# Where weights stand in TensorE: a high product of 512 columns as two of 256 in one half bank

## The chip, the cores and the metric

The kernel runs on one core of one Trainium2 chip. The metric is the device time of one execution in microseconds, given as the median of several runs; lower is better. One execution was also recorded by the profiler, and everything said about engines comes from that one.

## The reference

One decoder layer on 256 tokens of width 2048, in float32. Cut to what matters:

```python
h = rms_norm(x, g_mix)
z = h @ w_in                      # 2048 -> pool 512 | q-latent 512 | kv-latent 256 | rope key 64 | memory query 512
y = concat(pool_mixer(z_pool), mla(z_q, z_kv, z_kr), mem_attention(z_mq, mem)) @ w_o
x = x + y
h = rms_norm(x, g_ffn)
g, u = h @ w_gate, h @ w_up       # 2048 -> 5632 each
gc = conv_b + sum_j conv_w[j] * shift(g, j)        # causal, width 3
x = x + (silu(gc) * u) @ w_down   # 5632 -> 2048
```

## The kernel before

Every operand of a large product is split into two float32r parts, high and low, where low is the rest that high leaves. A product a x b is computed as high x high + high x low + low x high; the fourth term is left out. Weights arrive by DMA in blocks of 1 MB (load_w, tile wr) and are split by split_w: ACT casts to wh (L98), DVE subtracts to wl (L99), in pieces of 128 x 1024. Activations are split in the same way by split_act, and their high and low parts stand beside each other: xg[:, k, 0:256] and [256:512] in the input stage, h2[:, 0, k] and h2[:, 1, k] in the feed-forward stage.

There are two manners of product. In gemm_n (the memory keys and values, the query and rope key, the up-projections, the output projection) and in prod (the down-projection) the activations stand in TensorE as the stationary operand and weights stream past, mostly 512 columns. In gemm_t, gemm_z and gemm_pair the weights stand and the activations stream past: these three are where the change is. Their output is 128 features by 256 tokens, and a bank of PSUM has room for 512 columns. For each of the 16 blocks k of the inner dimension,

- a *high* product streams both parts of the activations, 512 columns, past the high weights: the product with high activations goes into the first half of the bank, that with low activations into the second half;
- a *low* product streams the high part of the activations, 256 columns, past the low weights into the second half.

The helper sides picks output and moving operand for both. Afterwards the two halves are added: ACT copies the first half to SBUF and DVE adds the second, in half_add (L509, L510, tile hadd) in the input stage and in halves (L809, L810, tiles g and u) in the feed-forward stage.

The stages in order of time, by the profile: the memory product, where memory keys and values are made (to about 50 us); the query and rope key (50 to 77 us); six latent blocks with gemm_z (L140), between whose high and low runs the steps of the memory attention are put (77 to 126 us); four pool blocks, the first with gemm_z and three with gemm_t (L124), among the up-projections (126 to 182 us); attention heads beside the output projection (to 288 us); the feed-forward stage; the down-projection (771 to 996 us).

The feed-forward stage loops over f, 44 blocks of 128 features. Each f takes two banks, for gate and up. The first f is done in two halves by gemm_t, with other work between. The other 43 use gemm_pair (L156): the gate's 16 high products, its 16 low ones, then the up's 16 low ones and its 16 high ones, so that runs of one kind meet, also across two f: TensorE sees 32 low, 32 high, 32 low, and so on. Then glu makes the result on ACT and DVE: add the halves of the gate, multiply by the row scale r1 (L815), convolve (L817, L819), silu (L820), add the halves of the up part, multiply (L826 or L834), split.

A scheduler places the instructions on each engine by dependency and priority; where keep() is called, they stay in the order of the program. Matmuls and splits of gemm_pair are not kept. Banks come from a pool of four (ps_main), the parts of weights from pools of four buffers each. The tile of the low weights has 64 spare columns, and its start is shifted by 48 columns for the first half of a block of weights and by 16 for the second.

Of the kernel before, what the change touches and what calls it, by code (L numbers as in the profile page):

```python
# [60 lines left out]
def layer(ctx, tc, xT_d, xn_d, memT_d, vec_d, tab_d, w_z_d, w_mqkr_d, w_q_d, w_kv_d, w_mem_d, w_pool_d, w_o_d,  # L61
          w_g_d, w_u_d, w_dn_d, out_d):
    nc = tc.nc
# [24 lines left out]
    def keep(ins, on=True):  # L88

        return tc.keep_in_program_order(ins) if on else ins  # L90
# [18 lines left out]
    def gemm_t(ps, raw, o, act, ks, first=True, last=True, kept=False, between=None):  # L109


        ks = list(ks)
        nk = HS // P
        cs = range(0, len(ks), nk)
        for c in cs:
            kc = ks[c:c + nk]

            hi, lo = split_w(raw, o + c * P, len(kc) * P, shift=16 if c // nk % 2 else 48)

            for low in ((False, True) if c // nk % 2 == 0 else (True, False)):  # L120
                for i, k in enumerate(kc):
                    w = (lo if low else hi)[:, i * P:(i + 1) * P]
                    out, m = sides(ps, act(k), low)
                    keep(nc.tensor.matmul(out, w, m,  # L124
                                          start=first and c + i == 0 and not low,
                                          stop=last and c == cs[-1] and i == len(kc) - 1 and low == (c // nk % 2 == 0),
                                          skip_group_check=True), kept)
            if between is not None and c == 0:
                between()

    def gemm_z(ps, raw, act, between, low_first):


        nk = HS // P
        parts = [split_w(raw, c * HS, HS, shift=16 if c else 48) for c in range(KD // nk)]
        for low in ((True, False) if low_first else (False, True)):
            for k in range(KD):
                i = k % nk
                o, m = sides(ps, act(k), low)
                keep(nc.tensor.matmul(o, parts[k // nk][low][:, i * P:(i + 1) * P], m, start=k == 0 and low == low_first,  # L140
                                      stop=k == KD - 1 and low != low_first, skip_group_check=True))
            if low == low_first:
                between()

    def gemm_pair(pss, raws, act):

        nk = HS // P
        for s, (ps, raw) in enumerate(zip(pss, raws)):


            parts = [split_w(raw, c * HS, HS, shift=16 if c else 48) for c in range(KD // nk)]
            for low in ((False, True) if s == 0 else (True, False)):
                for k in range(KD):
                    i = k % nk
                    o, m = sides(ps, act(k), low)
                    nc.tensor.matmul(o, parts[k // nk][low][:, i * P:(i + 1) * P], m,  # L156
                                     start=k == 0 and low == (s == 1), stop=k == KD - 1 and low == (s == 0),
                                     skip_group_check=True)

    def gemm_n(pss, hi, lo, act, k0, first, last, kept=False, by_span=False):  # L160

# [29 lines left out]
    def v(name, i=0):  # L191
        o = VOFF[name] + i
        return vec[:, o:o + 1]
# [309 lines left out]
        if m == 6:  # L503
            latent_scales()

    def half_add(dst, ps):

        t = mp.tile([P, T], F32, tag="hadd", name=nm("hadd"), bufs=3)
        nc.scalar.copy(t[:], ps[:, 0:T])  # L509
        nc.vector.tensor_tensor(dst, t[:], ps[:, T:2 * T], op=ALU.add)  # L510


    zl = mp.tile([P, 6, 2 * T], F32R, name="zl")
    zs = mp.tile([P, 2, T], F32, name="zs")

# [2 lines left out]
    for m in range(6):  # L518
        raw = load_w(w_z_d[m], STG)
        if m in (1, 3):  # L520
            keep(nc.sync.dma_start(x1n[:, m // 2, :], xn_d[m // 2]))
        ps = ps_main()
        gemm_z(ps, raw, lambda k: xg[:, k, :], lambda: mem_steps(m), m % 2 == 1)
        z = mp.tile([P, T], F32, tag="hadd", name=nm("z"), bufs=3)
        half_add(z[:], ps)
        a = zs[:, m // 4, :]
        if m % 4 == 0:
            nc.scalar.activation(a, z[:], AF.Square)
        else:
# [3 lines left out]
        split_act(zl[:, m, :], z[:], v("g_q_lat", m) if m < 4 else v("g_kv_lat", m - 4))  # L533


    sl, sl2 = sm(4), sm(4)
# [15 lines left out]
    zp = mp.tile([P, 4, T], F32, name="zp")  # L552
    def pool_in(g):
        raw = load_w(w_z_d[6 + g], STG)
        ps = ps_main()
# [247 lines left out]
    aT = {}  # L803
    hold = {}

    def halves(ps, tag):

        t = fp.tile([P, T], F32, tag=tag, name=nm(tag), bufs=1)
        nc.scalar.copy(t[:], ps[:, 0:T])  # L809
        nc.vector.tensor_tensor(t[:], t[:], ps[:, T:2 * T], op=ALU.add)  # L810
        return t

    def glu(f, psg, psu):
        g = halves(psg, "g")
        nc.vector.tensor_tensor(g[:], g[:], r1[:], op=ALU.mult)  # L815
        gc = fp.tile([P, T], F32, tag="gc", name=nm("gc"), bufs=1)
        nc.scalar.activation(gc[:], g[:], AF.Identity, bias=v("conv_b", f), scale=v("cw2", f))  # L817
        for d, w in ((1, "cw1"), (2, "cw0")):
            nc.vector.scalar_tensor_tensor(gc[:, d:T], g[:, 0:T - d], v(w, f), gc[:, d:T], op0=ALU.mult, op1=ALU.add)  # L819
        nc.scalar.activation(gc[:], gc[:], AF.Silu)  # L820
        u = halves(psu, "u")
        j, e = f // 2, f % 2
        if j not in SEVEN:
            if e == 0:
                aT[j] = fp.tile([P, 2, 2 * T], F32R, name=nm("aT"))
            nc.vector.tensor_tensor(u[:], u[:], gc[:], op=ALU.mult)  # L826
            split_act(aT[j][:, e, :], u[:])
            return
        if e == 0:
# [4 lines left out]
        nc.vector.tensor_tensor(s[:, o:o + 2, :].rearrange("p a t -> p (a t)"), u[:], gc[:], op=ALU.mult)  # L834
# [8 lines left out]


    raws = [load_w(w[0], STG) for w in (w_g_d, w_u_d)]
    pss = [ps_main() for _ in range(2)]
    for ps, raw in zip(pss, raws):
        gemm_t(ps, raw, 0, lambda k: h2[:, :, k, :], range(8), last=False)
    turn(3)
# [4 lines left out]
        gemm_t(ps, raw, HS, lambda k: h2[:, :, k, :], range(8, KD), first=False)  # L854
    glu(0, *pss)
    for f in range(1, KF):
        pss = [ps_main() for _ in range(2)]
        gemm_pair(pss, [load_w(w[f], STG) for w in (w_g_d, w_u_d)], lambda k: h2[:, :, k, :])
        glu(f, *pss)

# [191 lines left out]
```

## Time and profile before

| what | value |
|---|---|
| median of 3 runs | 1003.43 us (1003.19 to 1003.74) |
| span of the profiled execution, first to last instruction | 1001.9 us |
| TensorE matmuls | 5338, busy 996.0 us (99%) |
| TensorE weight loads | 5338, busy 857.8 us (86%) |
| DVE busy | 767.7 us (77%), 1160 instructions |
| ACT busy | 587.0 us (59%), 859 instructions |
| DMA | 200.17 MB, mean 200 GB/s |
| the loop of gemm_pair (L156) | 1376 high and 1376 low matmuls |

The page gives the span alone for the profiled execution; what lies before its first and after its last instruction is in the run's time and not in the span. In the groups of the profile a row names the line, the engine, the operation and the tiles (out<-in), the shape and the count; then, after the bar, the busy time in us and the mean duration of one in ns; then the idle time of the engine just before, with what ended it. In the timeline a row has the start in us, the length of a run of equal instructions, and their count. Matmuls are pipelined: the record of one lasts beyond the start of the next, so durations overlap and the distance between starts is what counts.

### The profile page before, as it was taken

The page shows a single profiled execution, that of the slowest core. Times are in us where ns is not written, and L with a number is a line of the kernel's source. Part 1 is how long each engine was busy: PE and PEld are TensorE (multiplying, and loading weights), DVE is VectorE, ACT ScalarE, POOL GpSimd, SP SyncE. Part 2 cuts the span into 40 slices and gives each one's busy share as a digit, 9 for nine tenths or more (in the row PEclk, how much of TensorE's full clock was granted, in tenths as well). Part 3 has the DMA queues.
Part 4 walks back from the last instruction along what each step waited for, and adds up shares of the span by engine and source line. Part 5 has one row for each costly group of instructions (what it writes and reads, how often), then busy time and mean ns, then how long its engine had stood idle before and what let it go on. Part 6 is the DMA issues. An engine that isn't in the chain of part 4 may idle for free.

```text
span 1001.9 us, 14016 instructions
## 1 busy us (share of the span) xinstructions
PE 996.0 (99%) x5338; PEld 857.8 (86%) x5338; DVE 767.7 (77%) x1160; ACT 587.0 (59%) x859; POOL 18.5 (2%) x39
## 2 busy tenths in 40 slices
PE   9999999999999999999999999999999999999998
PEld 7898888888888888888888888888888888888886
DVE  6778689855677767677767677777677898998997
ACT  7678666544576556555655565555565665545652
POOL 1010000000000000000000000000000000010000
PEclk9999999999999999999999999999999999999999
DMA  9867443433664555555555555555556655585651
GB/s 357 293 241 281 156 175 138 167 128 132 232 224 169 199 188 202 174 205 188 191 200 192 197 180 199 194 184 208 189 191 223 240 207 178 203 305 199 216 205 43
DMA packets 31764, 200.17 MB, mean 200 GB/s; under 512 B 3664, under 2 KB 4176, under 8 KB 9808
## 3 DMA queue, kind: packets, MB, share of 16 engines
q1 hardware_dynamic: 28512, 189.04, 52.8%
q0 software_dynamic: 2752, 9.44, 2.7%
q8 instruction: 42, 0.69, 0.3%
q10 hardware_dynamic: 432, 0.79, 0.2%
q14 instruction: 26, 0.21, 0.1%
HBM read 195.06 MB, written 4.19 MB: 199 GB/s over the span
## 4 chain that ended last, share of the span: by engine, by line
PE 99%; DVE 0%; issue 0%
PE psm L156 47%; PE psm L175 5%; PE psm L173 5%; PE psm L174 5%; PE psm L140 4%; PE psa L882 4%; PE psm L882 4%; PE psa L880 4%; PE psa L881 4%; PE psm L880 4%; PE psm L881 4%; PE psm L124 3%; PE psa L703 1%; PE psa L173 1%; PE psa L175 1%; PE psa L174 1%
## 5 line engine op out<-in xcount | busy, mean ns | idle before, releaser
L99 DVE TENSOR_TENSOR wl<-wr,wh 128x1024 fp32r<-128x1024 f32 (+2 forms) x338 | 390.5, 1170 | 133.7 <-ACT wh L98 76.0
L98 ACT CAST wh<-wr 128x1024 fp32r<-128x1024 f32 (+2 forms) x338 | 339.5, 1009 | 139.3 <-PE psm L156 55.4
L156 PE MATMUL psm<-h,wh 128*128 128x512 f32 x1376 | 320.1, 390 | 0.0
L156 PEld LDWEIGHTS psm<-h,wh 128*128 128x128 f32 x1376 | 255.1, 188 | 51.2
L156 PEld LDWEIGHTS psm<-h,wl 128*128 128x128 f32 x1376 | 163.8, 188 | 3.3
L156 PE MATMUL psm<-h,wl 128*128 128x256 f32 x1376 | 164.5, 277 | 0.0
L98 ACT CAST wh<-dn 128x1024 fp32r<-128x1024 f32 (+1 forms) x66 | 66.0, 1008 | 75.5 <-PE psa L881 35.1
L99 DVE TENSOR_TENSOR wl<-dn,wh 128x1024 fp32r<-128x1024 f32 (+1 forms) x66 | 75.0, 1164 | 15.8 <-ACT wh L98 15.8
L817 ACT ACTIVATE gc<-g,vec 128x256 f32<-128x256 f32 x44 | 26.5, 602 | 93.4 <-DVE g L815 93.4
L819 DVE SCALAR_TENSOR_TENSOR gc<-g,vec,gc 128x255 f32<-128x255 f32 x88 | 42.5, 483 | 33.0 <-ACT gc L817 31.4
L173 PE MATMUL psm<-wh,cat 128*128 128x512 f32 x96 | 38.2, 398 | 0.0
L175 PE MATMUL psm<-wl,cat 128*128 128x512 f32 x96 | 37.4, 390 | 0.0
L174 PE MATMUL psm<-wh,cat 128*128 128x512 f32 x96 | 37.4, 389 | 0.0
L881 PE MATMUL psa<-wh,aT 128*128 128x512 f32 x88 | 34.3, 390 | 0.0
L880 PE MATMUL psa<-wh,aT 128*128 128x512 f32 x88 | 34.3, 389 | 0.0
L881 PE MATMUL psm<-wh,aT 128*128 128x512 f32 x88 | 34.3, 389 | 0.0
L880 PE MATMUL psm<-wh,aT 128*128 128x512 f32 x88 | 34.2, 389 | 0.0
L882 PE MATMUL psa<-wl,aT 128*128 128x512 f32 x88 | 33.9, 389 | 0.0
L882 PE MATMUL psm<-wl,aT 128*128 128x512 f32 x88 | 33.9, 389 | 0.0
L809 ACT COPY g<-psm 128x256 f32<-128x256 f32 x44 | 16.5, 375 | 27.7 <-PE psm L156 27.7
L881 PE MATMUL psm<-wh,aS 128*128 128x512 f32 x77 | 30.0, 390 | 0.0
L881 PE MATMUL psa<-wh,aS 128*128 128x512 f32 x77 | 30.0, 390 | 0.0
(238 smaller groups left out, 1424.2 us busy)
## 6 DMA issues: line engine op xcount, KB each, us to landing
wr<-in_w_g SPq DMA_DIRECT2D x44, 1024.0 KB, 4.8
wr<-in_w_u SPq DMA_DIRECT2D x44, 1024.0 KB, 4.8
wr<-in_w_dn SPq DMA_DIRECT2D x33, 1024.0 KB, 4.9
wr<-in_w_o SPq DMA_DIRECT2D x16, 1024.0 KB, 4.8
dn<-in_w_dn SPq DMA_DIRECT2D x11, 1024.0 KB, 4.8
wr<-in_w_z SPq DMA_DIRECT2D x10, 1024.0 KB, 6.7
wr<-in_w_mem SPq DMA_DIRECT2D x6, 1024.0 KB, 8.4
wr<-in_w_mqkr SPq DMA_DIRECT2D x8, 576.0 KB, 5.2
```

The lines of the kernel that those rows point to most:

```text
L98: keep(nc.scalar.copy(hi[:, c:e], raw[:, o + c:o + e]), kept)
L99: keep(nc.vector.tensor_tensor(lo[:, c:e], raw[:, o + c:o + e], hi[:, c:e].bitcast(F32), op=ALU.subtract), kept)
L124: keep(nc.tensor.matmul(out, w, m, start=first and c + i == 0 and not low, stop=last and c == cs[-1] and i == len(kc) - 1 and low == (c // ...
L140: keep(nc.tensor.matmul(o, parts[k // nk][low][:, i * P:(i + 1) * P], m, start=k == 0 and low == low_first, stop=k == KD - 1 and low != lo ...
L156: nc.tensor.matmul(o, parts[k // nk][low][:, i * P:(i + 1) * P], m, start=k == 0 and low == (s == 1), stop=k == KD - 1 and low == (s == 0) ...
L173: keep(nc.tensor.matmul(ps, xh, hi[:, i, o], start=first and i == 0, stop=False), kept)
L174: keep(nc.tensor.matmul(ps, xl, hi[:, i, o], start=False, stop=False), kept)
L175: keep(nc.tensor.matmul(ps, xh, lo[:, i, o], start=False, stop=last and i == nk - 1), kept)
L819: nc.vector.scalar_tensor_tensor(gc[:, d:T], g[:, 0:T - d], v(w, f), gc[:, d:T], op0=ALU.mult, op1=ALU.add)
L880: nc.tensor.matmul(ps, a[0], b[0], start=first, stop=False)
L881: nc.tensor.matmul(ps, a[1], b[0], start=False, stop=False)
L882: nc.tensor.matmul(ps, a[0], b[1], start=False, stop=last)
```

## The change

In the three helpers in which weights stand, a high product becomes two matmuls of 256 columns with the same stationary block, one with the high and one with the low part of the activations. Both add into the first half of the bank, where the low product adds too. The helper rounds gives the moving operands, two for a high product and one for a low one. All callers pass ps_main()[:, 0:T]. The second half of the bank is no longer used, so half_add and halves are gone: the squares, split_act and the multiplications by rxb, r1 and gc read the bank in PSUM directly. The tile u is now only made for pairs that are not in SEVEN; the tag hadd (three buffers) gives way to zsq (two).

```diff
-    def sides(ps, m, low):
-        if len(m.shape) == 3:
-            return (ps[:, T:2 * T], m[:, 0]) if low else (ps[:].rearrange("p (a t) -> p a t", a=2), m)
-        return (ps[:, T:2 * T], m[:, 0:T]) if low else (ps[:, 0:2 * T], m)
+    def rounds(act, k, low):
+        m = act(k)
+        h, l = (m[:, 0], m[:, 1]) if len(m.shape) == 3 else (m[:, 0:T], m[:, T:2 * T])
+        return (h,) if low else (h, l)
...
     def gemm_pair(pss, raws, act):
...
-                    o, m = sides(ps, act(k), low)
-                    nc.tensor.matmul(o, parts[k // nk][low][:, i * P:(i + 1) * P], m,
-                                     start=k == 0 and low == (s == 1), stop=k == KD - 1 and low == (s == 0),
-                                     skip_group_check=True)
+                    for a, m in enumerate(rounds(act, k, low)):
+                        nc.tensor.matmul(ps, parts[k // nk][low][:, i * P:(i + 1) * P], m,
+                                         start=k + a == 0 and low == (s == 1), stop=k == KD - 1 and low == (s == 0),
+                                         skip_group_check=True)
...
-    def half_add(dst, ps):
-        t = mp.tile([P, T], F32, tag="hadd", name=nm("hadd"), bufs=3)
-        nc.scalar.copy(t[:], ps[:, 0:T])
-        nc.vector.tensor_tensor(dst, t[:], ps[:, T:2 * T], op=ALU.add)
...
-        ps = ps_main()
+        ps = ps_main()[:, 0:T]
         gemm_z(ps, raw, lambda k: xg[:, k, :], lambda: mem_steps(m), m % 2 == 1)
-        z = mp.tile([P, T], F32, tag="hadd", name=nm("z"), bufs=3)
-        half_add(z[:], ps)
...
-            nc.scalar.activation(a, z[:], AF.Square)
+            nc.scalar.activation(a, ps, AF.Square)
         else:
-            t = mp.tile([P, T], F32, tag="hadd", name=nm("zsq"), bufs=3)
-            nc.scalar.activation(t[:], z[:], AF.Square)
+            t = mp.tile([P, T], F32, tag="zsq", name=nm("zsq"), bufs=2)
+            nc.scalar.activation(t[:], ps, AF.Square)
...
-        half_add(zp[:, g, :], ps)
-        nc.vector.tensor_tensor(zp[:, g, :], zp[:, g, :], rxb[:], op=ALU.mult)
+        nc.vector.tensor_tensor(zp[:, g, :], ps, rxb[:], op=ALU.mult)
...
-    def halves(ps, tag):
-        t = fp.tile([P, T], F32, tag=tag, name=nm(tag), bufs=1)
-        nc.scalar.copy(t[:], ps[:, 0:T])
-        nc.vector.tensor_tensor(t[:], t[:], ps[:, T:2 * T], op=ALU.add)
-        return t
-
     def glu(f, psg, psu):
-        g = halves(psg, "g")
-        nc.vector.tensor_tensor(g[:], g[:], r1[:], op=ALU.mult)
+        g = fp.tile([P, T], F32, tag="g", name=nm("g"), bufs=1)
+        nc.vector.tensor_tensor(g[:], psg, r1[:], op=ALU.mult)
...
-        u = halves(psu, "u")
...
-            nc.vector.tensor_tensor(u[:], u[:], gc[:], op=ALU.mult)
+            u = fp.tile([P, T], F32, tag="u", name=nm("u"), bufs=1)
+            nc.vector.tensor_tensor(u[:], psu, gc[:], op=ALU.mult)
```

gemm_t and gemm_z are changed in the same way as gemm_pair.

More of the change, by code (lines that the diff above doesn't have):

```diff
@@ L116, in gemm_t @@
             kc = ks[c:c + nk]
-            hi, lo = split_w(raw, o + c * P, len(kc) * P, shift=16 if c // nk % 2 else 48)
-            for low in ((False, True) if c // nk % 2 == 0 else (True, False)):
+            parts = split_w(raw, o + c * P, len(kc) * P, shift=16 if c // nk % 2 else 48)
+            lows = (False, True) if c // nk % 2 == 0 else (True, False)
+            for low in lows:
                 for i, k in enumerate(kc):
[L122 to L127, printed above, removed]
+                    for a, m in enumerate(rounds(act, k, low)):
+                        nc.tensor.matmul(ps, parts[low][:, i * P:(i + 1) * P], m,
+                                         start=first and c + i + a == 0 and not low,
+                                         stop=last and c == cs[-1] and i == len(kc) - 1 and low == lows[1],
+                                         skip_group_check=True)
             if between is not None and c == 0:
@@ L138, in gemm_z @@
                 i = k % nk
-                o, m = sides(ps, act(k), low)
-                keep(nc.tensor.matmul(o, parts[k // nk][low][:, i * P:(i + 1) * P], m, start=k == 0 and low == low_first,
-                                      stop=k == KD - 1 and low != low_first, skip_group_check=True))
+                for a, m in enumerate(rounds(act, k, low)):
+                    keep(nc.tensor.matmul(ps, parts[k // nk][low][:, i * P:(i + 1) * P], m,
+                                          start=k + a == 0 and low == low_first,
+                                          stop=k == KD - 1 and low != low_first, skip_group_check=True))
             if low == low_first:
```

15 lines of the change are left out of this document (8 added, 7 removed).

## The prediction

> **What bounds the kernel now.** I read the busy line of the page first, then the chain that ended last, then the waits of TensorE, then the timeline of TensorE alone inside the long stage.
>
> ```profile
> span 1001.9 us, 14016 instructions
> PE 996.0 (99%) x5338; PEld 857.8 (86%) x5338; DVE 767.7 (77%) x1160; ACT 587.0 (59%) x859; POOL 18.5 (2%) x39
> PEclk9999999999999999999999999999999999999999
> PE 99%; DVE 0%; issue 0%
> 300.87 470.43 PE psm L156 x2752
> PE psa L294 <- DVE eps L201: 1.1, 1, 1.1
> ```
>
> The chain is TensorE for 99% of the span, and its only listed wait is 1.1 us before its first matmul. The granted clock never leaves the top digit. One line, the loop of gemm_pair (L156), holds 470.43 us in one piece. So the time is the number of matmuls times the distance between their starts, and nothing else is worth anything unless it makes TensorE wait. A matmul's own duration does not give that distance, because successive matmuls overlap:
>
> ```profile
> L156 PE MATMUL psm<-h,wh 128*128 128x512 f32 x1376 | 320.1, 390 | 0.0
> L156 PE MATMUL psm<-h,wl 128*128 128x256 f32 x1376 | 164.5, 277 | 0.0
> ```
>
> By mean durations (390 and 277 ns) two of 256 would cost 554 against 390, which is not what happens: 1376 x (390 + 277) ns would be 918 us, and the stage takes 470. The starts in the timeline of TensorE give the distance:
>
> ```profile
> 315.29 3.83 PE L156 MATMUL psm<-h,wl 128*128 128x256 f32 x32
> 318.95 7.44 PE L156 MATMUL psm<-h,wh 128*128 128x512 f32 x32
> 326.23 3.83 PE L156 MATMUL psm<-h,wl 128*128 128x256 f32 x32
> 329.89 7.44 PE L156 MATMUL psm<-h,wh 128*128 128x512 f32 x32
> ```
>
> The pattern repeats every 10.94 us (one f). 32 low products take 318.95 - 315.29 = 3.66 us, 114.4 ns each; 32 high products take 326.23 - 318.95 = 7.28 us, 227.5 ns each. Two low distances are 228.8 ns. That is the whole dispute: 1.3 ns per high product, or about half a per cent of a high block.
>
> Inside a block the distance is not even. Windows cut from the two blocks (start, length, count; length less one duration, over count less one):
>
> ```profile
> 315.29 0.99 PE L156 MATMUL psm<-h,wl 128*128 128x256 f32 x7
> 317.02 2.09 PE L156 MATMUL psm<-h,wl 128*128 128x256 f32 x17
> 318.95 1.55 PE L156 MATMUL psm<-h,wh 128*128 128x512 f32 x6
> 321.70 4.69 PE L156 MATMUL psm<-h,wh 128*128 128x512 f32 x20
> ```
>
> At the head of the low block (0.99 - 0.277)/6 = 119 ns, later (2.09 - 0.277)/16 = 113.3. At the head of the high block (1.55 - 0.390)/5 = 232 ns, later (4.69 - 0.390)/19 = 226.3. So each change between high and low costs a short run-in: 3.66 - 32 x 0.1133 = 0.034 us in the low block and 7.28 - 32 x 0.2263 = 0.038 us in the high one. Once settled, 2 x 113.3 = 226.6 against 226.3: columns are paid for, instructions hardly.
>
> **The change part by part.** *Matmuls.* 1568 high products (1376 in L156, 112 in L140, 48 + 32 in L124) become two of 256 columns each; the columns streamed stay the same. TensorE gets 6906 matmuls and 6906 weight loads instead of 5338. Rows for the other two lines:
>
> ```profile
> 95.05 3.63 PE psm L140 x32
> 100.84 7.32 PE psm L140 x32
> 115.31 7.27 PE psm L140 x32
> 131.46 1.98 PE L124 MATMUL psm<-xg,wh 128*128 128x512 f32 x8
> 133.27 2.01 PE L124 MATMUL psm<-xg,wl 128*128 128x256 f32 x16
> 135.12 1.77 PE L124 MATMUL psm<-xg,wh 128*128 128x512 f32 x7
> ```
>
> L140: 113.4 ns per low product, 227 to 229 per high. L124, in its short blocks: high (133.27 - 131.46)/8 = 226 ns, low (135.12 - 133.27)/16 = 115.6, so two low distances are 5 ns more than a high one there.
>
> The cost of the split is bounded by two readings of these rows. Settled distances: 226.6 - 226.3 = 0.3 ns on the 1488 products of L156 and L140, 0.4 us; with 80 of L124 at 5 ns, 0.4 us, the sum is +0.8 us. Block means, run-ins counted once per instruction: 1.3 ns x 1568 = +2.0 us. Below nothing: the run-in might come from the change of width, which disappears, since all matmuls of the stage will be 256 wide; then 43 x (0.034 + 0.038) = -3.1 us. Against that, the windows show a run-in both from wide to narrow and from narrow to wide, and the tile of weights changes at the same places, so I leave one run-in per change of tile. I take +0.8 us, because 57 of the 64 high matmuls of a block will lie behind its head, where the settled row is the nearest; I keep -3.1 and +2.0 as ends.
>
> *A repeated weight load.* The second half of a high product loads the same 128x128 block again. In the page the loads equal the matmuls (5338 and 5338), although the kernel already has neighbours with one stationary block (in plain, the last product of one n and the first of the next), so no load is skipped, and none will be.
>
> ```profile
> 318.84 7.13 PEld L156 LDWEIGHTS psm<-h,wh 128*128 128x128 f32 x32
> 326.01 3.85 PEld L156 LDWEIGHTS psm<-h,wl 128*128 128x128 f32 x32
> ```
>
> The low block runs one load per 256 columns without falling behind (32 loads in 3.85 us, the 32 matmuls in 3.83), so the same rate in a high block is already on show, for 3.66 us at a stretch. The Trainium skill, page "TensorE: Matmul & The Clock Gate", section "LDWEIGHTS (loading the stationary operand)", puts a load at columns over 1.2 GHz, by estimate 106.7 ns for 128 columns; that would still fit under a distance of 113.3 ns, though with 6% to spare instead of half, and the low block agrees with it.
>
> *ACT and DVE work taken away.* Rows of the long stage, then of the two input stages:
>
> ```profile
> L809 ACT COPY g<-psm 128x256 f32<-128x256 f32 x43 | 16.1, 375 | 27.7 <-PE psm L156 27.7
> L809 ACT COPY u<-psm 128x256 f32<-128x256 f32 x43 | 16.0, 373 | 17.7 <-PE psm L156 17.7
> L810 DVE TENSOR_TENSOR g<-g,psm 128x256 f32<-128x256 f32 x44 | 18.3, 416 | 0.0
> L810 DVE TENSOR_TENSOR u<-u,psm 128x256 f32<-128x256 f32 x43 | 17.8, 415 | 0.0
> L509 ACT COPY hadd<-psm 128x256 f32<-128x256 f32 x10 | 3.8, 375 | 5.3 <-PE psm L140 3.1 <-PE psm L124 2.2
> L510 DVE TENSOR_TENSOR z<-hadd,psm 128x256 f32<-128x256 f32 x6 | 2.5, 419 | 0.0
> L510 DVE TENSOR_TENSOR zp<-hadd,psm 128x256 f32<-128x256 f32 x4 | 1.7, 417 | 0.9 <-ACT hadd L509 0.9
> ACT wh L98 <- PE psm L156: 55.4, 85, 0.9
> ```
>
> About 36 us of ACT and 40 us of DVE go. All of it lies beside TensorE, and the last row shows the direction of the wait: the cast that makes the next weights waits for TensorE to give back a buffer, 85 times, never the reverse. Value taken: 0. In the input stages the results come 0.8 us earlier (375 + 419 ns), but TensorE has no wait listed there; bound 0 to -1 us, from the two short waits of transposes:
>
> ```profile
> PEld psa L266 <- DVE tok L654: 0.7, 2, 0.5
> PEld psa L266 <- DVE tok L599: 0.6, 2, 0.4
> ```
>
> Neither tile comes from a half_add, so I take 0 of this too. The cover is the weight splits' slack: if it were lost, the loss would appear as TensorE waiting for wh or wl.
>
> *Operands moved to PSUM.* The multiply by r1 or rxb, the squares and split_act now read the bank itself. Reading PSUM costs DVE no more than SBUF here:
>
> ```profile
> L815 DVE TENSOR_TENSOR g<-g,r 128x256 f32<-128x256 f32 x44 | 18.7, 425 | 1.1
> ```
>
> (425 ns without PSUM, 416 with.) A bank is held longer: in glu until the product with gc instead of the copy. Four banks with two per f leave a bank a whole f, 10.94 us, before it is wanted again, while the chain from the copy of g to the product takes 323.67 + 0.42 - 317.34 = 6.75 us:
>
> ```profile
> 317.34 0.37 ACT L809 COPY g<-psm 128x256 f32<-128x256 f32 x1 [0.80 <-PE psm L156]
> ...
> 323.67 0.42 DVE L834 TENSOR_TENSOR s<-u,gc 128x256 f32<-128x256 f32 x1
> ```
>
> In the input stages three readers instead of two hold a bank about 1 us longer, with four banks and one in use. Cost 0. The waits for the banks move on DVE and ACT; queued behind them is the next weight split, with the slack named above. No DMA, and no queue of SP or POOL, is touched.
>
> *Sum.* 0.8 + 0 + 0 = +0.8 us on a span of 1001.9 us. The median of the runs is 1003.43, 1.5 us above the span (what lies before the first and after the last instruction; unchanged). Forecast 1003.4 + 0.8 = 1004.2 us, no change: a measurement of this kernel can tell about 0.2%, 2.0 us, from nothing.
>
> **The rivals.** *The split blocks never settle (slower).* The settled distance of 113.3 ns is shown for wl as weights and for one run of moving blocks; a high block has weights in wh, and its moving operand jumps between the high and low half of the activations at each matmul. If that keeps it in the state of a block's head, 119 ns, the price is 2 x 119 - 227.5 = 10.5 ns x 1568 = 16 us, 1020 us; if half the products stay there, 8 us, 1011 us. It decides (2 us) once one product in eight stays unsettled. For it: the heads exist, and a short low block (115.6 ns in L124) is partly in that state. Against: the 512-wide blocks settle with the same wh and both halves, and the low blocks settle across the change from one wl buffer to the next.
>
> *A fixed cost per matmul.* The line through the block means (114.4 at 256 columns, 227.5 at 512) has 1.3 ns per matmul at no columns: +2.0 us, 1005.4 us, at the edge of slower; if the distances at the heads count for more, up to 1007. The same page of the Trainium skill, section "Wait — 56ns, not 53.3ns?", gives a warm matmul a fixed 2.5 ns beside its columns; by that rule 1568 more matmuls would cost by estimate 3.9 us, and 1007.3 us would come out. The settled rows here (0.3 ns) do not agree with it.
>
> *Run-ins vanish and the input stage tightens (faster).* 43 x 0.072 = 3.1 us, and up to 1 us of earlier transposes: 1003.4 - 3.1 = 1000.3, at the least 999.3. For it: the long stage becomes one width. Against: the tiles still change. It decides once two thirds of the run-ins go.
>
> *ACT and DVE relief counts after all.* If weights did reach TensorE late, its waits would list it; they don't. I give this nothing of its own.
>
> **How the numbers follow.** Forecast (settled to block-mean distances, 1002.5 to 1005.4 us): 0.60. Unsettled blocks: 0.18, half of it above 1011. Fixed cost beyond the means: 0.12, 1005.4 to 1007.5. Run-ins vanish: 0.10. So faster 0.10, no change 0.60, slower 0.30. The likeliest case alone spans 1002.5 to 1005.4. The range reaches down to 1001.0, two thirds of the run-ins gone, and up to 1011.0, where half the products stay unsettled; outside lie about 0.05 below and 0.09 above.
>
> **What would show it.** In the timeline of TensorE a high block becomes 64 matmuls of 256; right if the start of the next block is 7.24 to 7.32 us later, wrong if 7.5 or more (unsettled) or the period of 10.94 us changes by over 0.05. Loads and matmuls 6906 each. ACT and DVE busy down by about 36 and 40 us with no new row of TensorE waiting for wh, wl or a bank. A wait of TensorE for DVE's reading of a bank would make the holding argument wrong; a shift in the stretch from 77 to 182 us alone would mean that the order of work around the input stages changed.

## The result, and the profile after

The changed kernel takes 1021.53 us (1021.44 to 1021.61, four runs) against 1003.59 us (1003.19 to 1003.83) for the kernel before on the same chip: a ratio of 1.0179, with a 95% interval of 1.0167 to 1.0191. It is slower by 17.9 us. The forecast was no change, 1004.2 us.

The page of the changed kernel: the busy line, the chain that ended last, and the costliest groups.

```profile
span 1019.6 us, 16975 instructions
PE 1013.8 (99%) x6906; PEld 939.0 (92%) x6906; DVE 726.8 (71%) x1062; ACT 556.9 (55%) x761; POOL 18.5 (2%) x39
PE 98%; DVE 1%; ACT 1%; issue 0%; ACTq 0%
L156 PE MATMUL psm<-h,wh 128*128 128x256 f32 x2752 | 337.4, 283 | 0.0
L156 PEld LDWEIGHTS psm<-h,wh 128*128 128x128 f32 x2752 | 333.1, 192 | 0.0
L156 PE MATMUL psm<-h,wl 128*128 128x256 f32 x1376 | 163.0, 276 | 0.0
L156 PEld LDWEIGHTS psm<-h,wl 128*128 128x128 f32 x1376 | 159.5, 188 | 0.0
```

TensorE is still busy for 99%, with 6906 matmuls and 6906 loads. DVE and ACT have given up 40.9 and 30.1 us. One thing is odd: matmuls of one line and one shape, 256 columns, last 283 ns with wh as weights and 276 ns with wl, and their loads 192 and 188 ns. TensorE's list of waits, complete:

```profile
PE psa L294 <- DVE eps L201: 1.1, 1, 1.1
PE psa L786 <- DVE h L186: 0.2, 1, 0.2
```

So TensorE waits for nothing new but 0.2 us. The long stage in the chain, with its start and length, which was 300.87 and 470.43 before:

```profile
303.41 486.18 PE psm L156 x4128
```

It is 15.75 us longer. It also starts 2.54 us later, and what follows it takes 230.0 us instead of 230.6; 15.75 + 2.54 - 0.6 = 17.7 us, the whole difference of the spans. The timeline of TensorE inside the stage, and then the same stretches by windows (length, busy time with the records touched, granted clock, DMA share and GB/s):

```profile
322.02 7.84 PE L156 MATMUL psm<-h,wh 128*128 128x256 f32 x64
329.70 3.79 PE L156 MATMUL psm<-h,wl 128*128 128x256 f32 x32
333.32 7.84 PE L156 MATMUL psm<-h,wh 128*128 128x256 f32 x64
```

```profile
322.02:329.70 7.68, 7.68 (x67) 1.00 0.51 155
329.70:333.32 3.62, 3.62 (x34) 1.00 0.63 256
```

64 halves of high products take 7.68 us, 120.0 ns each; 32 low products take 3.62 us, 113.1 ns (113.3 by the starts of single matmuls). Both are at granted clock 1.00, so it is not the clock. A high product went from 227.5 to 2 x 120.0 = 240.0 ns, +12.5 ns x 1376 = +17.2 us; a low one went from 114.4 to 113.3 ns, -1.5 us. That is 15.7 of the measured 15.75 us. Ahead of the stage, 192 more high products (112 + 80) at the same +12.5 ns would make 2.4 of the 2.54 us. The question for the experiments was why the same operation, 256 columns with one weight load, costs 113.3 ns with wl and 120.0 ns with wh.

### The profile page after: what moved, and what is told of

It reads as the page before. It is cut to its first block, busy times and chain, and to the rows that moved or that the text cites. A ratio compares the mean times of both kernels' runs of the same rounds, so it can differ in the third digit from the quotient of the medians.

```text
span 1019.6 us, 16975 instructions
## 1 busy us (share of the span) xinstructions
PE 1013.8 (99%) x6906; PEld 939.0 (92%) x6906; DVE 726.8 (71%) x1062; ACT 556.9 (55%) x761; POOL 18.5 (2%) x39
## 4 chain that ended last, share of the span: by engine, by line
PE 98%; DVE 1%; ACT 1%; issue 0%; ACTq 0%
PE psm L156 48%; PE psm L173 5%; PE psm L175 5%; PE psm L174 5%; PE psm L139 4%; PE psa L865 4%; PE psm L865 4%; PE psa L863 4%; PE psa L864 4%; PE psm L863 4%; PE psm L864 4%; PE psm L123 2%; PE psa L693 1%; PE psa L173 1%; PE psa L175 1%; PE psa L174 1%
## 5 line engine op out<-in xcount | busy, mean ns | idle before, releaser
L156 PE MATMUL psm<-h,wh 128*128 128x256 f32 x2752 | 337.4, 283 | 0.0
L156 PEld LDWEIGHTS psm<-h,wh 128*128 128x128 f32 x2752 | 333.1, 192 | 0.0
L156 PEld LDWEIGHTS psm<-h,wl 128*128 128x128 f32 x1376 | 159.5, 188 | 0.0
L803 ACT ACTIVATE gc<-gc 128x256 f32<-128x256 f32 x44 | 18.4, 418 | 62.3 <-DVE gc L802 62.3
```

The costliest lines, as they stand in the source:

```text
L156: nc.tensor.matmul(ps, parts[k // nk][low][:, i * P:(i + 1) * P], m, start=k + a == 0 and low == (s == 1), stop=k == KD - 1 and low == (s ...
```

## The experiments

Each ratio is to the kernel before, run on the same chip. Four suspects were left by the result: the stationary block that is loaded twice in a row, the moving operand that jumps between the halves of h2, the changed work of ACT and DVE, and the place of the tiles in SBUF. The last came from the code: wl has its columns shifted by 48 or 16, wh has none. By the addresses of the built program the high weights and the activations then begin at the same byte modulo 512 (192), while the two shifts of wl put it at 384 and 0, 192 and 320 bytes away.

**low_aligned.** The kernel before, with no jump and no repeat; only the low weights move to where wh stands relative to the activations.

```diff
-shift=16 if c else 48     # gemm_t, gemm_z, gemm_pair
+shift=64 if c else 0
```

> The kernel before, with one edit: the low weights are shifted by 0 and 64 columns instead of 48 and 16, so that by the built program's own placement they begin at the same byte modulo 512 as the activations that stream past, as the high weights do in both kernels (with 48 and 16 they begin 192 or 320 bytes away). Theory A, place: 256-wide matmuls start 120 ns apart where weights and moving columns begin at the same byte modulo 512, and 113.3 ns where they begin 192 or 320 bytes apart. Then the low blocks here go from 3.66 to 3.84 us for 32, and the time from 1003.6 to 1003.6 + 1568 x (120 - 114.4) ns = 1012 us. Theory B, the same weights loaded twice in a row cost time, and theory C, the moving operand that jumps between the high and the low half at each matmul costs time: neither occurs here, so 1003.6 us and 3.66 us.

Measured 1011.69 us (1011.31 to 1012.08), ratio 1.008 (1.0063 to 1.0097). Its timeline:

```profile
327.51 4.00 PE L156 MATMUL psm<-h,wl 128*128 128x256 f32 x32
331.35 7.44 PE L156 MATMUL psm<-h,wh 128*128 128x512 f32 x32
338.63 4.00 PE L156 MATMUL psm<-h,wl 128*128 128x256 f32 x32
```

331.35 - 327.51 = 3.84 us for 32 low products, 120.0 ns: the loss appears without the change, on the other tile. The 512-wide high block beside it keeps its 7.28 us.

**high_shifted.** The changed kernel, with the high weights shifted as the low ones are.

```diff
-hi = stage.tile([P, HS], F32R, tag="wh", ...)
+hi = stage.tile([P, HS + 64], F32R, tag="wh", ...)[:, shift:shift + HS]
```

> The kernel after, with one edit: the tile of the high weights gets 64 spare columns and the same shift of 48 and 16 columns as the low weights. Theory A (place): a high block of 64 goes from 7.68 to 7.25 us, the time from 1021.5 to 1021.5 - 3136 x 6.7 ns = 1000.5 us, which is under the kernel before (1003.6). Theories B (repeated weights) and C (jumping moving operand): unchanged, 7.68 us and 1021.5 us.

Measured 1002.10 us (1001.88 to 1002.48, ten runs), ratio 0.9986 (0.9977 to 0.9996): 19.4 us less than the changed kernel, and a little less than the kernel before. The group, the timeline and the windows:

```profile
L156 PE MATMUL psm<-h,wh 128*128 128x256 f32 x2752 | 319.1, 276 | 0.0
```

```profile
320.06 7.42 PE L156 MATMUL psm<-h,wh 128*128 128x256 f32 x64
327.31 3.79 PE L156 MATMUL psm<-h,wl 128*128 128x256 f32 x32
```

```profile
320.06:327.31 7.25, 7.25 (x66) 1.00 0.50 157
```

7.25 / 64 = 113.3 ns, with every block still loaded twice and the halves still alternating; the duration falls from 283 to 276 ns. A displacement of the high weights by 48 and 16 columns, in a tile widened by 64 to make room for it, removes the whole loss in the stage, which takes 467.84 us instead of 486.18. In all it saves 1.6 us less than was expected: ahead of the stage the gain is 1.3 us (the stage starts at 302.09 instead of 303.41), where 384 halves at 6.7 ns would make 2.6.

**halves_apart.** The changed kernel, with all products with high activations of a block first, then all with low ones: no block is loaded twice in a row, no operand jumps.

```diff
-for low in ((False, True) if s == 0 else (True, False)):
+for low, r in (((False, 0), (False, 1), (True, 0)) if s == 0 else ((True, 0), (False, 0), (False, 1))):
...
-for a, m in enumerate(rounds(act, k, low)):
+for a, m in enumerate(rounds(act, k, low)[r:r + 1]):
```

> The kernel after, with one edit in gemm_pair alone: a high block streams first all 16 high activations past the 16 high weights, and then all 16 low activations, so that no weights are loaded twice in a row and the moving operand does not jump at each matmul. Theory A (place): unchanged, 120 ns and 1021.5 us. Theories B and C: 113.3 ns, a block of 64 in 7.25 us, the time 1021.5 - 2752 x 6.7 ns = 1003 us.

Measured 1021.40 us (1021.33 to 1021.71), ratio 1.0179 (1.0164 to 1.0194).

```profile
322.30 7.84 PE L156 MATMUL psm<-h,wh 128*128 128x256 f32 x64
329.98 3.79 PE L156 MATMUL psm<-h,wl 128*128 128x256 f32 x32
```

329.98 - 322.30 = 7.68 us, as in the changed kernel. Neither the repeated load nor the jump costs anything.

**sweep_256.** One execution of the changed kernel, with the high tile widened as in high_shifted, that gives each f a shift of its own, for both tiles and both halves of a block of weights, to read a distance for each place.

```diff
+SHIFTS = [*range(0, 64, 2), 1, 3, 5, 7, 9, 15, 31, 33, 47, 49, 63]   # one for each f of gemm_pair
...
-parts = [split_w(raw, c * HS, HS, shift=16 if c else 48) for c in range(KD // nk)]
+parts = [split_w(raw, c * HS, HS, shift=shift) for c in range(KD // nk)]
```

> The kernel after, with the tile of the high weights widened as in high_shifted, and in gemm_pair another shift for each f: 0, 2, 4 ... 62 columns for f = 1 to 32, then 1, 3, 5, 7, 9, 15, 31, 33, 47, 49, 63. The two halves of a block of weights lie in buffers 256 bytes apart modulo 512, so that all distances in bytes between weights and moving columns come up in steps of 8. Theory A (place): the distance between starts changes from f to f, 120 ns near shift 0 in the first half, 113.3 ns at 16 and 48. Theories B and C: 120 ns in high blocks and 113.3 ns in low blocks for every f.

One execution took 1022.54 us. Low blocks of shift 0, 2 and 16 in its timeline, each with the start of the block after it:

```profile
306.03 4.00 PE L157 MATMUL psm<-h,wl 128*128 128x256 f32 x32
309.88 7.71 PE L157 MATMUL psm<-h,wh 128*128 128x256 f32 x64
317.42 3.86 PE L157 MATMUL psm<-h,wl 128*128 128x256 f32 x32
321.12 7.65 PE L157 MATMUL psm<-h,wh 128*128 128x256 f32 x64
...
396.62 3.79 PE L157 MATMUL psm<-h,wl 128*128 128x256 f32 x32
400.25 7.58 PE L157 MATMUL psm<-h,wh 128*128 128x256 f32 x64
```

The starts give 3.85, 3.70 and 3.63 us for 32 products: 120.3, 115.6 and 113.4 ns. The other places lie between these ends; in this execution shifts 16 and 22 alone settled at 113.3 to 113.4, shift 48 (half of what high_shifted uses) stood at 117.8 instead of the expected 113.3, and the same shift gave the same distance in high and low blocks. So the distance is neither one of two values nor a matter of the tile's kind. Nor is it the wider tile that cures high_shifted: shift 0 has it here and stays at 120.

**shift_16_all.** The best place of the sweep, everywhere and always: both tiles, both halves, shift 16.

> The kernel after, with the tiles of both parts of the weights shifted by 16 columns for both halves of a block of weights (in gemm_t, gemm_z and gemm_pair). In the sweep, an f with this shift ran at 113.3 ns in high and low blocks, one with 48 at 117.8. Theory A (place): the stage of gemm_pair at 113.3 ns as in high_shifted, and in the input stages no slow stretch of some 14 matmuls with shift 48 ahead of the 16, about 10 stretches x 14 x 4.5 ns = 0.6 us: 1002.1 - 0.6 = 1001.5 us. Rival: the alternation of 48 and 16 is what lets TensorE settle; then 115 ns or more, 1004 us and above.

The twelve runs fell into two groups: five at 1001.73 to 1001.98 us and seven at 1020.17 to 1020.62 us, one program at one granted clock (0.999 to 1.00). The ratio of the first group is 0.9983 (0.9972 to 0.9994). The profiled run is of the second (1020.41 us):

```profile
317.18 3.93 PE L156 MATMUL psm<-h,wl 128*128 128x256 f32 x32
320.95 7.70 PE L156 MATMUL psm<-h,wh 128*128 128x256 f32 x64
328.49 3.93 PE L156 MATMUL psm<-h,wl 128*128 128x256 f32 x32
```

7.54 us for 64 and 3.77 us for 32, 117.8 ns each, through the whole stage. The first group has no trace; its times lie some 18.5 us lower, which over the 4128 matmuls of the stage is 4.5 ns each, so by estimate it ran at 113.3. Neither expectation holds for all twelve runs. A place can have two distances, then, and the execution that was traced kept its one for hundreds of microseconds.

**sweep_again.** The same sweep in another order, with 16 four times, 22 three times, and places not tried yet.

> The sweep once more, with the shifts in another order and others among them (f = 1 to 43: 22, 16, 50, 0, 48, 2, 62, 26, 12, 56, 36, 4, 16, 22, 16, 60, 8, 40, 17, 21, 23, 11, 13, 19, 25, 27, 29, 35, 37, 39, 41, 43, 45, 51, 53, 55, 57, 59, 61, 52, 15, 22, 16). Theory A (place): each shift has the distance of the first sweep, within 0.5 ns, wherever it stands: 16 and 22 113.3, 50 116.7, 2 115.6, 62 117.7, 0, 26, 36 and 60 120. Rival, history: the distance is left over from the f before, or is a matter of chance, and the same shift gives other values than in the first sweep, by several ns.

One execution took 1019.50 us. Low blocks of shift 16 as the second f, shift 0, shift 16 as the 13th f, and shift 27, each with the start of the next block:

```profile
317.04 3.93 PE L157 MATMUL psm<-h,wl 128*128 128x256 f32 x32
320.81 7.68 PE L157 MATMUL psm<-h,wh 128*128 128x256 f32 x64
...
339.62 4.00 PE L157 MATMUL psm<-h,wl 128*128 128x256 f32 x32
343.46 7.63 PE L157 MATMUL psm<-h,wh 128*128 128x256 f32 x64
...
440.90 3.79 PE L157 MATMUL psm<-h,wl 128*128 128x256 f32 x32
444.52 7.42 PE L157 MATMUL psm<-h,wh 128*128 128x256 f32 x64
...
586.80 4.08 PE L157 MATMUL psm<-h,wl 128*128 128x256 f32 x32
590.71 7.89 PE L157 MATMUL psm<-h,wh 128*128 128x256 f32 x64
```

Shift 16 stands at 3.77 us (117.8 ns) and later at 3.62 (113.1); as the 15th and 43rd f it is at 113.3 again. Shift 48 went from 117.8 in the first sweep to 113.3, shift 22 from 113.4 to 116.7 in one of three places, and shifts 4, 26, 36 and 60 moved by 1.7 to 2.6 ns. Shift 0 is at 120 in both sweeps, and 2, 8, 12, 50, 56 and 62 also repeat within 0.1 ns. The slowest place is new: shift 27 takes 3.91 us, 122.2 ns. The expectation that each place keeps its distance within 0.5 ns is refuted. The place narrows the distance down; whether what ran before decides the rest, or chance, these runs do not separate.

**moving_shifted.** The changed kernel, with the high weights left alone, the low ones of gemm_pair at shift 64, and the activations displaced by 48 columns instead, so that the distance between weights and activations is, modulo 256 bytes, that of shift 16.

```diff
-h2 = big.tile([P, 2, KD, T], F32R, tag="act", name="h2")
+h2 = big.tile([P, 2 * KD * T + 64], F32R, tag="act", name="h2")[:, 48:48 + 2 * KD * T]
...
-shift=16 if c else 48
+shift=64
```

> The kernel after, with the high weights where they were (shift 0), and the activations of the feed-forward stage moved by 48 columns instead; the low weights of gemm_pair get a shift of 64. Between weights and moving columns this is the distance of a shift of 16. If the place of the one against the other decides: 113.3 ns in gemm_pair, a block of 64 in 7.25 us, and 1021.5 - 2752 x 6.7 ns = 1003.1 us. If the place of the weights alone decides, high blocks stay at 120 ns, 7.68 us and 1021.5 us or more.

Measured 1021.80 us (1021.69 to 1022.00), ratio 1.0181 (1.0166 to 1.0195).

```profile
322.45 7.70 PE L156 MATMUL psm<-h,wh 128*128 128x256 f32 x64
329.98 3.93 PE L156 MATMUL psm<-h,wl 128*128 128x256 f32 x32
333.75 7.70 PE L156 MATMUL psm<-h,wh 128*128 128x256 f32 x64
```

The time is that of the changed kernel, but the parts are not: the high block fell from 7.68 to 7.53 us, the low block rose from 3.62 to 3.77 (117.8). This is the second distance of shift 16. So the place of the activations seems to count too, since untouched high weights left 120; but the better distance was not reached.

**sweep_512.** The kernel before, with a shift for each f in both tiles and the high products still 512 wide.

> The kernel before (high products of 512 columns), with the tile of the high weights widened, and in gemm_pair the shifts of the first sweep, f by f. The low blocks should repeat that sweep: 113.3 ns at 16 and 22, 120 at 0 and 26. For the high blocks: if a bad place costs per weight load, at worst 6.7 ns more in 226.7; if it costs per column, up to 240 ns; if 512-wide products always settle, 226.7 at every shift. Known so far is 226.7 at shift 0, where 256-wide ones run at 120 ns.

One execution took 1015.15 us. The low block of shift 0 and the high block behind it, half of shift 0 and half of shift 2; then shift 14's high block, half of it of shift 16:

```profile
304.89 4.00 PE L157 MATMUL psm<-h,wl 128*128 128x256 f32 x32
308.72 7.51 PE L157 MATMUL psm<-h,wh 128*128 128x512 f32 x32
316.07 3.88 PE L157 MATMUL psm<-h,wl 128*128 128x256 f32 x32
...
387.28 7.62 PE L157 MATMUL psm<-h,wh 128*128 128x512 f32 x32
394.73 3.93 PE L157 MATMUL psm<-h,wl 128*128 128x256 f32 x32
```

At 512 the good and bad places are others. Shift 0, among the worst at 256, is among the best here: taken apart by the starts of single matmuls its products average 227 to 229 ns, while most other shifts give 231 to 234 (394.73 - 387.28 = 7.45 us, 232.8 ns). A common loss of 6 to 7 ns per matmul at 512 is of the size seen at 256, so it does not grow with the columns. The low blocks did not all repeat the first sweep, as was expected: shift 16 is at 117.8 here instead of 113.3, shift 26 at 117.8 instead of 120.

**before_high_shifted.** That reading tested whole: the kernel before with the shift that cures the changed one.

> The kernel before (high products of 512 columns), with the high weights shifted by 48 and 16 columns as the low ones are. In the sweep of that kernel single shifts mostly gave 231 to 233 ns for a high product and shift 0 gave 227 to 230. If alternating 48 and 16 settles 512-wide products as it does 256-wide ones: 226.7 ns and 1003.5 us. If 512 columns want the place that they have: 232 ns, 1003.5 + 1568 x 5 ns = 1011 us.

Measured 1015.56 us (1015.43 to 1016.01), ratio 1.0121 (1.0106 to 1.0137).

```profile
327.01 3.94 PE L156 MATMUL psm<-h,wl 128*128 128x256 f32 x32
330.79 7.60 PE L156 MATMUL psm<-h,wh 128*128 128x512 f32 x32
338.23 3.94 PE L156 MATMUL psm<-h,wl 128*128 128x256 f32 x32
```

7.44 / 32 = 232.5 ns for a high product and 3.78 / 32 = 118.1 for a low one. The same displacement that saves 19.4 us with 256-wide high products costs 12 us with 512-wide ones, and it takes the low products, whose own place is unaltered, out of 113.3 as well: the blocks beside them seem to count too.

**adds_kept.** high_shifted with the removed kind of work put back on ACT and DVE in the feed-forward stage: one copy and one pass of 128 x 256 for each g and u, 88 of each.

> high_shifted, with ACT and DVE given back in glu the work that the change takes away: an ACT copy of the bank to SBUF and one more DVE pass over 128 x 256 (the maximum of the tile with itself, which changes no value), for gate and up, 88 times each. If that work is hidden beside TensorE, as the prediction took it: 1002.1 us as high_shifted, period of one f 10.88 us. Rival: the shorter path on ACT and DVE is where the gain of high_shifted over the kernel before comes from; then 1003.5 us, or the period grows by up to 0.8 us an f (35 us).

Measured 1002.13 us (1001.93 to 1002.55, eleven runs), ratio 0.9987 (0.9978 to 0.9996), against 1002.10 without. Its busy line:

```profile
PE 994.5 (99%) x6906; PEld 919.6 (92%) x6906; DVE 761.4 (76%) x1150; ACT 576.4 (58%) x849; POOL 18.5 (2%) x39
```

36 us of DVE and 20 us of ACT more than in high_shifted (725.0 and 556.6), and the time is the same. The relief of these two engines is worth nothing here.

**places_0_56** and **query_shifted.** high_shifted with another pair of places that alternate, 0 and 56; and high_shifted with the 576-column pieces of the query stage displaced as well.

```diff
-shift=16 if c else 48     # places_0_56
+shift=56 if c else 0
...
-hi, lo = split_w(raw, i * 576, 576)     # query_shifted
+hi, lo = split_w(raw, i * 576, 576, shift=16 if i else 48)
```

> high_shifted with the shifts 0 and 56 in place of 48 and 16. Neither 0 (120 ns) nor 56 (116.7 ns) was seen at 113.3 ns in any sweep; 48 and 16 were seen both at 113.3 and at 117.8. If any alternation of two places sets TensorE free: 113.3 ns, 1002 us. If at least one of the places must have 113.3 ns among its states: 116.7 to 120 ns, 1002.1 + 4704 x 3.3 to 6.7 ns = 1018 to 1033 us.

> high_shifted, and the pieces of 576 weights of the query stage (50 to 77 us, where activations stand and weights stream past, 288 columns) shifted by 48 and 16 as well. That stage runs at 133 ns a matmul in every trace so far, 16 cycles in 15 more than the rate of the settled stages (113.3 / 256 x 288 = 127.5 ns). If the place matters there too: 192 x 5.8 ns = 1.1 us less, 1001.0 us. If 288 columns never settle: 1002.1 us.

places_0_56 took 1023.84 us (1023.79 to 1024.04), ratio 1.0203 (1.0189 to 1.0217):

```profile
322.42 7.74 PE L156 MATMUL psm<-h,wh 128*128 128x256 f32 x64
329.99 3.95 PE L156 MATMUL psm<-h,wl 128*128 128x256 f32 x32
```

7.57 / 64 = 118.3 ns on average, and single distances run from 113 to 121: alternation by itself does not settle the stream. query_shifted took 1001.99 us (1001.82 to 1002.44, eleven runs), ratio 0.9986 (0.9977 to 0.9994), no different from high_shifted. Most of the 288-wide matmuls of that stage stayed at 130 to 136 ns (median 132 against 133); 22 of 189 starts were 126 to 128 ns apart, against 4. The expectation's own figures make 133 ns 4% more than 127.5, and not 16 in 15.

**moving_alternates** and **moving_alternates_512.** The changed kernel, high weights undisplaced, with the low weights of gemm_pair as in the cut below and the activations at one place for k below 8 and another above, so that the distance between weights and activations alternates as in high_shifted: modulo 256 bytes in the first, modulo 512 in the second.

```diff
+def h2k(k):
+    o = k * T + (16 if k < KD // 2 else 48)     # 48 and 80 in the second
+    return h2[:, :, o:o + T]
...
-shift=16 if c else 48
+shift=64                                        # 64 if c else 0 in the second
```

> The kernel after with its high weights where they were (shift 0); the activations of the feed-forward stage are laid 16 columns further for the first eight blocks of the inner dimension and 48 further for the last eight, and the low weights of gemm_pair get a shift of 64. Between weights and moving columns these are, modulo 256 bytes, the distances of high_shifted in high and low blocks alike, and no weight tile alternates. If the place of the one against the other decides: 113.3 ns in gemm_pair, a period of 10.88 us, and 1002.1 us plus at most 2 us for the high blocks of the input stages, which stay at 120 ns: 1002 to 1004 us. If the place of the weights alone decides: high blocks at 120 ns, 1021 us.

> The kernel after with its high weights where they were (shift 0) and, in gemm_pair, the low weights at the same place as they; the activations of the feed-forward stage are laid 48 columns further for the first eight blocks of the inner dimension and 80 further for the last eight, with room so that both halves of the activations keep that place. Now the distances between weights and moving columns are 192 and 320 bytes modulo 512, the two of high_shifted (there in the order 320, 192), where moving_alternates had them modulo 256 only, and came to 117 ns. If the distance modulo 512 decides: 113.3 ns, a period of 10.88 us, 1002 to 1004 us. If the place of each by itself matters, or what ran before: 117 to 120 ns, 1017 to 1022 us.

Both took 1018.98 us (1018.98 to 1019.26 and 1018.90 to 1019.06), ratios 1.0156 (1.0139 to 1.0173) and 1.0154 (1.0137 to 1.0171). The first one's timeline:

```profile
322.11 7.64 PE L156 MATMUL psm<-h,wh 128*128 128x256 f32 x64
329.59 3.93 PE L156 MATMUL psm<-h,wl 128*128 128x256 f32 x32
333.36 7.64 PE L156 MATMUL psm<-h,wh 128*128 128x256 f32 x64
```

7.48 / 64 = 116.9 ns for a half of a high product: between the two; the second run has the same 7.48 us. By single starts, part of a block runs at 113 to 114 ns and the rest mostly at 117 to 119. The low blocks of the first run are the sharpest case. By the addresses their weights lie 192 and 320 bytes from the activations modulo 512, for the same eight blocks k as in the kernel before, where the settled distance is 113.3 ns; here it is 3.77 / 32 = 117.8. The relative distance between weights and activations, by itself, is therefore not the rule: distances like those of high_shifted (in the second run the same two modulo 512, in the other order), made by moving the activations, save 2.5 us of the 19.4.

## Why the prediction was wrong, point by point

*What bounds the kernel.* Right: TensorE, by the number of matmuls times the distance between starts. The whole result is in that product.

*The cost of the split.* This is the step that failed. It took the settled 113.3 ns from low products, whose weights stand in wl with a shift, and used it for high products, whose weights stand in wh without one; the settled 226.3 ns of 512-wide products with wh was taken as evidence that wh is as good. No row of the kernel before shows a 256-wide product with wh, and the runs show that neither half of the inference holds: the place that is good at 512 (shift 0, 227 ns) is among the worst at 256 (120 ns, in the changed kernel, in low_aligned and in both sweeps), and the pair that is good at 256 is bad at 512 (232.5 ns in before_high_shifted). The term came out as +12.5 ns for each of 1568 products, 19.6 us, where +0.8 us in all was written; the run-ins then gave 1.5 us back. Had the upper bound been drawn from the slowest 256-wide row on show (119 ns at the head of a low block), the range would have reached 1020 us, still 1.5 us short of the result.

*The rival that came true.* "The split blocks never settle" was priced at 119 ns and 1020 us with a chance of 0.18, and half of that chance lay above 1011. Its price was nearly right (120.0 ns, 1021.5 us), and so was the place of the loss, the high blocks. That the price came from the head of a low block is luck as far as the runs go: none shows that a head and a bad place are the same thing. Of its two reasons one is refuted: the jump between the halves costs nothing (halves_apart). The other, that wh is the weight tile, was right, but not for being the high tile: low_aligned has the same 120 ns with wl. The argument that spoke against it, that 512-wide blocks settle with the same wh, does not carry over to 256.

*A repeated weight load.* Right: 6906 loads, none skipped, and no cost; high_shifted runs 64 of them in 7.25 us. The Trainium skill, page "TensorE: Matmul & The Clock Gate", section "Step-by-step: what each phase is for", says that the weight load and the moving operand have read ports of their own, so that loading the next weights takes nothing from the running matmul. The distance of 113.3 ns fits it. In other places the same instructions lie up to 122.2 ns apart (shift 27 in sweep_again, clock 1.00), and no run shows whether it is the load that costs the time there. What is shown is that the place matters, not which part of the chip is shared.

*A fixed cost per matmul.* Rightly held unlikely: two halves in high_shifted take 2 x 113.3 = 226.6 ns, as much as one settled matmul of 512. By the fixed 2.5 ns per matmul of the Trainium skill, page "TensorE: Matmul & The Clock Gate", section "Wait — 56ns, not 53.3ns?", the split of the stage's 1376 products would cost 3.4 us, an estimate. The trace does not agree: the stage of high_shifted is 2.6 us shorter than before.

*ACT and DVE.* Right that it is hidden (adds_kept). DVE fell by 40.9 us where 40 was written, ACT by 30.1 where 36 was: the records of ACT overlap their neighbours, so that busy time counts a copy for less than its duration; adds_kept puts 88 of some 370 ns back, 33 us, and ACT's busy time rises by 20. The bound of 1 us for the input stages was a little low by its own rows, which add up to 1.3 us; nothing rests on it.

*Operands in PSUM and the banks.* Right: no wait of TensorE for a bank appeared, and the multiply of g that now reads PSUM takes 417 ns against 425.

```profile
L798 DVE TENSOR_TENSOR g<-psm,r 128x256 f32<-128x256 f32 x44 | 18.4, 417 | 1.6 <-issue 1.6
```

*Run-ins.* The rival that let them vanish was right in what it said and too small to see beside the loss: with all matmuls 256 wide the low block goes from 3.66 to 3.62 us although the tile of weights still changes at its ends, which was the prediction's reason to keep the run-ins; and in high_shifted the period of one f is 10.88 us instead of 10.94, 43 x 0.06 = 2.6 us, which is the stage's gain (470.43 to 467.84 in the chain). 1.2 us of it is lost again ahead of the stage, which starts at 302.09 us instead of 300.87. By the starts of single matmuls, 1.0 us of that lies in the high products of gemm_z and gemm_t, 46.6 us in all instead of 45.5; why was not followed.

*What stays open.* Why a place costs what it does; no view shows a bank or a port. What makes an execution take one of two distances in the same place (shift_16_all, sweep_again). Why moving the activations does not do what moving the weights does: three runs tried it, and none reached 113.3 throughout. Why the distance of the low products changed when only the high weights beside them were displaced (before_high_shifted). Shown are three things: the loss is in the distance between starts of 256-wide matmuls; it goes by displacing the high weights alone; and it comes without the split by displacing the low weights alone.

## What to carry to other kernels

A distance between matmuls belongs to a width and to the place of the operands, not to a width alone, and even then it can have two values: take it from a row with the same weight tile, the same displacement and the same width, and where none exists bound it at least by the worst row of that width (here 119 ns, where 120.0 came). An unexplained displacement in the code, on one tile and not on its neighbour, may be there because a distance depended on it; when a matmul's width changes, try the displacement of its weights again before judging the change. Here the split alone was 1.8% slower, and the split with displaced weights (high_shifted) 0.14% faster than the kernel before (0.04 to 0.23%).

## What the runs showed of the hardware that was not expected

- With one weight load for each matmul of 256 columns, the distance between starts ranged from 113.3 to 122.2 ns (averages of blocks) at a granted clock of 1.00, as the weights or the moving columns were displaced in SBUF. With 512 columns it ranged from 227 to 235 ns, and other places were the good ones.
- A stream can keep one of two distances for a whole stage: one program took 1001.7 to 1002.0 us in five runs and 1020.2 to 1020.6 us in seven, with the same granted clock; the traced one, of the seven, has 117.8 ns from end to end of the stage.
- Loading the same stationary block twice in a row costs nothing beside the streaming of 256 columns: 7.68 us for a block of 64 with it and without it (halves_apart), and 113.3 ns a matmul with it in high_shifted. It saves nothing either.
